# One queue of attention lines, the compression's small networks as its steps, and 128-row operands from the compressed probabilities

## Chip, cores and metric

One core of one Trainium2 chip. The metric is the device time of one execution in microseconds (us); the table below has the three runs of the kernel before.

## The reference

Two layers on 256 tokens of width 1024, all in float32. A layer is a gated feed-forward, an attention block, a second feed-forward and a small gated addition, each with an RMS norm ahead:

```python
h = h + 0.5 * swiglu(rms_norm(h, norm_g[i, 0]), ffn1_wi[i], ffn1_wo[i])
n = rms_norm(h, norm_g[i, 1])
... = split_cols(n @ w_in[i], IN_SPLITS)
ya = diff_attention(...)      # A: 4 heads, difference of two softmaxes
yb = nsa_attention(...)       # B: 8 heads in 2 groups, below
yc = swa_sink_attention(...)  # C: 8 heads in 2 groups, window 128, sinks
merged = (sigmoid(ga) * (ya @ w_branch[i, 0]) + sigmoid(gb) * (yb @ w_branch[i, 1])
          + sigmoid(gc) * (yc @ w_branch[i, 2]))
h = h + merged @ w_out[i]
```

Attention B has three parts that its gates sum: attention over compressed keys (15 blocks of 32 tokens at stride 16), over selected blocks (here all of them) and over a window. The compression is a small network, for keys and for values:

```python
def compress(t, pos, w1, w2):
    ...                                        # blocks of 32 tokens, + pos
    return jax.nn.gelu(blk @ w1) @ w2          # 15 rows of 64 a group
p_c = masked_softmax(s_c, dist_c >= 0)
o_c = einsum('bgrqn,bngd->bqgrd', p_c, v_cmp)  # joins o_s and o_w by gates
```

## The kernel before

**Products.** Every large product (`product`, L275) has the tokens, turned, as the stationary operand (128 x 128) and the weights as the moving one (128 x 512), with both split into a high and a low part: three matmuls a step (`mul3`, L218). Weights come in sub-blocks of 128 x 1024 through one queue (`Weights`, `fetch`, `load`, L232 to L264): a DMA, ScalarE's copy to `wh` (L212), VectorE's difference to `wl` (L207). Four raw buffers and six pairs of `wh` and `wl` go round.

**Lines beside the products.** The attentions A, C and B are generators, cut into steps by `yield`. `Flow` (L152) holds one of them. Each step of a product ends in `flow.tick()`, which adds the line's pace (0.75, 0.6, 0.7 for A, C, B; L33) and lets as many steps of the line be written as have come due. `flow.join` writes what is left. So a line's instructions stand between the product's in program order. A planner in the framework then sets each engine's order: by program order, but it takes a later instruction where an earlier one isn't ready by its reckoning. On the chip each engine's order is fixed.

**Order of a layer's attention block** (L873 to L896): projections A0, A1, A2; line A starts; projections Ck, Cq, Bk (16 ticks each); join; line C starts; Bv, Bq (16 each); branch 0, that is for each half c of the output columns a gate product (16 ticks) and a branch product (8); join; line B starts; `compress` (L604, 32 ticks); branch 2 the same way as branch 0; branch 1 with both gates first, then a join, then both branch products; then `wo`.

**Line B** (`attend_b`, L712) has six units: for tokens t = 0 the groups g = 0 and 1, for t = 1 each group twice (selected, window). `first` makes scores (L439), softmax (L448, L450) and scaling (L742); `second` turns the probabilities (L227), splits them into `pT` (L212, L207) and multiplies with the values (`weighted`, L664 and L665); `gather` (L669 to L676) adds halves and writes `yB`. The first and second of neighbouring units alternate (`pipelined`, L464). Ahead of the first second of each t stands `attend_cmp` (L680), whose turned probabilities `pcT` (L706 to L709, 16 rows) and compressed values `vc` (L654 to L659, 16 rows) make the last product of each g and t (L748). While `kc` is missing the line's steps are empty (L735).

**compress** makes 64 matmuls with `w1` (L624, L625), copies the sums to `c_sb` (L628), folds (L631), and runs the GELU and the second layer (L632 to L660) at one go, with `w2` from the weights' queue.

Of the kernel before, what the change touches and what calls it, by code (L numbers as in the profile page):

```python
# [10 lines left out]
F32 = mybir.dt.float32  # L11
# [123 lines left out]
def _constants():  # L135
    u = np.arange(REV)
    dist = 255 - u
    n = np.maximum(dist, 0)
    nf = np.maximum(n, 1).astype(np.float32)
    big = 16 + (np.log(nf / np.float32(16)) / np.float32(math.log(MAXDIST / 16)) * np.float32(16)).astype(np.int32)  # L140
    bucket = np.where(n < 16, n, np.minimum(big, BUCKETS - 1))
    onehot = (bucket[None, :] == np.arange(BUCKETS)[:, None]).astype(np.float32)
    dead = np.zeros((NB, REV), np.float32)
    dead[:, dist < 0] = NEG
    dead[12:, dist >= 128] = NEG
    ql, t, m = np.arange(128)[:, None, None], np.arange(2)[None, :, None], np.arange(16)[None, None, :]
    cmask = ((128 * t + ql - 16 * m - 31 >= 0) & (m < 15)).astype(np.float32).reshape(128, 32)
    return {"onehot": onehot, "dead": dead, "cmask": cmask, "ident": np.eye(128, dtype=np.float32),
            "fold": np.tile(np.eye(32, dtype=np.float32), (2, 1))}


class Flow:  # L152


    def __init__(self):
        self.side, self.pace, self.due = None, 0.0, 0.0

    def start(self, side, pace):
        self.side, self.pace, self.due = side, pace, 0.0

    def tick(self):
        if self.side is not None:
            self.due += self.pace
            while self.due >= 1.0:
                self.due -= 1.0
                if next(self.side, self) is self:
                    self.side = None
                    return

    def join(self):  # L170
        if self.side is not None:
            for _ in self.side:
                pass
            self.side = None


@with_exitstack
def trunk(ctx: ExitStack, tc: tile.TileContext, a: dict, out: bass.AP, index: list):
# [228 lines left out]
    def attention(i, norm, after):  # L407
# [193 lines left out]
        w1 = w2 = None  # L601
        kc, vc = [None], [None]

        def compress():  # L604
# [14 lines left out]
            for kv in range(2):  # L619
                for k in range(16):  # L620
# [5 lines left out]
                    flow.tick()  # L626
            c_sb = stage()
            nc.vector.tensor_copy(c_sb[:64], c_ps[:64])  # L628
            g_ps = tp_bank("gl")[:, :128]
            for k in range(4):  # L630
                nc.tensor.matmul(g_ps[:, 32 * k:32 * k + 32], c_sb[:64, 128 * k:128 * k + 128], fold, start=True, stop=True)  # L631
            gl = pool.tile([128, 128], F32, name="gl")  # L632
            nc.scalar.activation(gl, g_ps, AF.Square)
            nc.vector.tensor_scalar(gl, gl, 0.044715, 1.0, op0=ALU.mult, op1=ALU.add)
            nc.vector.tensor_tensor(gl, gl, g_ps, op=ALU.mult)
            nc.scalar.activation(gl, gl, AF.Tanh, scale=math.sqrt(2.0 / math.pi))
            nc.vector.tensor_scalar(gl, gl, 0.5, 0.5, op0=ALU.mult, op1=ALU.add)
            nc.vector.tensor_tensor(gl, gl, g_ps, op=ALU.mult)
            hid = pool.tile([128, 2, 128], F32R, name="hid")
            split(hid[:, 0], hid[:, 1], gl)  # L640
            w2h, w2l = w2(0)
            k_ps = tp_bank("kc")
# [8 lines left out]
            kt = pool.tile([128, 2, 2, 32], F32R, name="kc")  # L651
            split(kt[:, 0], kt[:, 1], kbd)
            v_ps = tp_bank("vc")
# [26 lines left out]
        def attend_cmp(t):  # L680
# [31 lines left out]
        def attend_b():  # L712
            bnd, y_ps = {}, {}

            def first(u):
# [107 lines left out]

        def branch(b, yT, last=False):

# [50 lines left out]
        yield project("A2", done_av)  # L876
        yield lambda: flow.start(attend_a(), PACE_A)
# [57 lines left out]
    fold = base.tile([64, 32], F32, name="fold")  # L935
    cmask = base.tile([128, 2, 16], F32, name="cmask")
    nsink = base.tile([128, DEPTH, 8], F32, name="nsink")
    nlam = base.tile([128, DEPTH], F32, name="nlam")
# [13 lines left out]
    def setup(pool):  # L952
# [14 lines left out]
        for g in range(2):  # L967
# [90 lines left out]
```

## Time and profile before

| what | value |
|---|---|
| runs, us | 1377.45, 1379.99, 1382.30; median 1379.99 |
| profiled execution, us | 1380.55 |
| its span, us | 1378.8 |
| TensorE (PE) busy | 1356.1 us, 98% of the span, 6598 matmuls |
| VectorE (DVE) busy | 882.2 us, 64% |
| ScalarE (ACT) busy | 779.1 us, 57% |
| granted TensorE clock, mean | 0.993 of full speed |
| HBM traffic | 183 GB/s over the span |

The profiled execution is one run. Its span goes from the first to the last instruction, and 1.75 us of its time lie around the span. Matmuls are pipelined, so that a record (0.39 us for a 128 x 512 product) is longer than the distance from one start to the next; costs are read from start to start. The attention block of layer 0 goes from 200 to 460 us; that of layer 1 repeats it 679 us later.

### The profile page before, as it was taken

How to read it: one execution, taken by the hardware profiler on the slowest of the kernel's cores; microseconds unless marked ns; L12 is line 12 of the kernel's file. 1: busy time of each engine (PE TensorE's matmuls, PEld its weight loads, DVE VectorE, ACT ScalarE, POOL GpSimd, SP SyncE). 2: the span in 40 equal slices, each digit the busy share in tenths (PEclk: the TensorE clock that was granted, in tenths of full speed). 3: DMA queues.
4: the chain of work that ended last, by engine and by line, in shares of the span. 5: the costliest groups of instructions: out<-in, count | busy, mean ns of one | idle time of the engine just before them, and what ended most of it. 6: DMA issues, size and time to landing. Idle time of an engine off the chain costs nothing.

```text
span 1378.8 us, 18265 instructions
## 1 busy us (share of the span) xinstructions
PE 1356.1 (98%) x6598; PEld 1111.2 (81%) x6598; DVE 882.2 (64%) x1585; ACT 779.1 (57%) x1377; POOL 19.1 (1%) x37
## 2 busy tenths in 40 slices
PE   7999999999999999999999999999999999999997
PEld 5888888887877888888888888888887778888886
DVE  6546556778877755555665555667697876555564
ACT  7535445668655644444654544566785656444454
POOL 0000000000000000000000000000000000000000
PEclk9999999999999999999999999999999999999999
DMA  8587566345634555555555555744546434555462
GB/s 284 189 268 241 192 205 211 122 160 169 223 119 137 165 186 184 183 173 187 199 183 183 183 183 176 243 157 132 169 164 221 139 123 166 195 183 188 161 205 87
DMA packets 74152, 249.53 MB, mean 181 GB/s; under 512 B 8720, under 2 KB 14276, under 8 KB 73934
## 3 DMA queue, kind: packets, MB, share of 16 engines
q1 hardware_dynamic: 73598, 243.36, 52.8%
q0 software_dynamic: 464, 5.01, 1.1%
q8 instruction: 52, 0.85, 0.2%
q14 instruction: 38, 0.31, 0.1%
HBM read 247.26 MB, written 5.01 MB: 183 GB/s over the span
## 4 chain that ended last, share of the span: by engine, by line
PE 92%; DMA 3%; DVE 3%; ACT 2%; issue 1%; SPq 0%; DVEq 0%; POOLq 0%; POOL 0%; ACTq 0%
PE ff L221 11%; PE ff L219 11%; PE ff L220 11%; PE fo L220 6%; PE fo L219 6%; PE fo L221 6%; PE gate L219 3%; PE gate L220 3%; PE gate L221 3%; DMA raw<-in_wst 2%; PE s L439 2%; PE br L219 2%; PE A L219 2%; PE A L220 2%; PE A L221 2%; PE br L221 2%
## 5 line engine op out<-in xcount | busy, mean ns | idle before, releaser
L207 DVE TENSOR_TENSOR wl<-raw,wh 128x1024 fp32r<-128x1024 f32 (+1 forms) x452 | 543.2, 1207 | 212.2 <-ACT wh L212 197.4
L212 ACT ACTIVATE wh<-raw 128x1024 fp32r<-128x1024 f32 (+1 forms) x452 | 471.0, 1046 | 218.1 <-PE fo L221 83.3
L219 PE MATMUL ff<-wh,nT 128*128 128x512 f32 x704 | 281.5, 400 | 6.7 <-ACT wh L212 6.7
L221 PE MATMUL ff<-wh,nT 128*128 128x512 f32 x704 | 277.6, 395 | 0.0
L220 PE MATMUL ff<-wl,nT 128*128 128x512 f32 x704 | 275.8, 392 | 0.0
L219 PEld LDWEIGHTS ff<-wh,nT 128*128 128x128 f32 x704 | 133.0, 189 | 33.7 <-ACT wh L212 7.4
L221 PEld LDWEIGHTS ff<-wh,nT 128*128 128x128 f32 x704 | 132.9, 189 | 27.5
L220 PEld LDWEIGHTS ff<-wl,nT 128*128 128x128 f32 x704 | 133.2, 189 | 26.9 <-DVE wl L207 0.9
L220 PE MATMUL fo<-wl,gT 128*128 128x512 f32 x352 | 134.3, 393 | 0.0
L221 PE MATMUL fo<-wh,gT 128*128 128x512 f32 x352 | 133.5, 390 | 0.0
L219 PE MATMUL fo<-wh,gT 128*128 128x512 f32 x352 | 133.3, 390 | 0.0
L388 ACT ACTIVATE act<-ff,stats 128x256 f32<-128x256 f32 x88 | 41.6, 473 | 159.1 <-PE ff L221 159.1
L389 DVE TENSOR_TENSOR gated<-act,ff 128x256 f32<-128x256 f32 x88 | 36.6, 416 | 124.2 <-ACT act L388 124.1
L219 PE MATMUL gate<-wh,nT 128*128 128x512 f32 x192 | 79.6, 414 | 0.0
L220 PE MATMUL gate<-wl,nT 128*128 128x512 f32 x192 | 78.4, 408 | 0.8 <-DVE wl L207 0.8
L221 PE MATMUL gate<-wh,nT 128*128 128x512 f32 x192 | 77.8, 405 | 0.0
L219 PEld LDWEIGHTS fo<-wh,gT 128*128 128x128 f32 x352 | 66.1, 188 | 13.7
L220 PEld LDWEIGHTS fo<-wl,gT 128*128 128x128 f32 x352 | 66.1, 188 | 13.4
L221 PEld LDWEIGHTS fo<-wh,gT 128*128 128x128 f32 x352 | 66.1, 188 | 13.3
L450 ACT ACTIVATE p<-p,st 128x128 f32<-128x128 f32 (+1 forms) x128 | 56.7, 446 | 12.1 <-DVE st L448 12.0
L305 ACT ACTIVATE nT<-nt,ngt 128x128 fp32r<-128x128 f32 x112 | 32.0, 371 | 31.1 <-PE nt L227 31.1
L220 PEld LDWEIGHTS gate<-wl,nT 128*128 128x128 f32 x192 | 37.6, 196 | 9.7 <-DVE wl L207 1.5
(286 smaller groups left out, 1961.3 us busy)
## 6 DMA issues: line engine op xcount, KB each, us to landing
raw<-in_wst SPq DMA_DIRECT2D x436, 512.0 KB, 4.3
band<-rev SPq DMA_DIRECT2D x10, 512.0 KB, 5.3
rev<-table POOLq DMA_DIRECT2D x1, 3840.0 KB, 17.3
raw<-in_wst SPq DMA_DIRECT2D x8, 256.0 KB, 6.0
raw<-in_wbv SPq DMA_DIRECT2D x4, 420.0 KB, 3.2
xt<-in_xt SPq DMA_DIRECT2D x4, 256.0 KB, 4.4
h<-in_x SPq DMA_DIRECT2D x2, 512.0 KB, 6.3
band<-rev POOLq DMA_DIRECT2D x2, 512.0 KB, 5.9
```

Of the source, the lines that this page charges most:

```text
L207: nc.vector.tensor_tensor(o, x, y, op=ALU.subtract)
L212: nc.scalar.activation(hi, src, AF.Copy)
L219: nc.tensor.matmul(ps, xh, wh, start=start, stop=False)
L220: nc.tensor.matmul(ps, xh, wl, start=False, stop=False)
L221: nc.tensor.matmul(ps, xl, wh, start=False, stop=stop)
L305: nc.scalar.activation(T[:, 0, k + m, :], src[:, 128 * m:128 * m + 128], AF.Copy, scale=ngt[:, self.row, k + m:k + m + 1])
L388: nc.scalar.activation(act, ps[:, :256], AF.Silu, scale=norm.r(t))
L389: nc.vector.tensor_tensor(held[t][:, f % 2, :], act, ps[:, 256:], op=ALU.mult)
L439: nc.tensor.matmul(o, q[r, x, qb[m], t * 128:(t + 1) * 128], kk, start=x + y == 0, stop=x == 1)
L450: nc.scalar.activation(p[j], p[j], AF.Exp, bias=st[:, j:j + 1], scale=-1.0, accum_out=st[:, n + j:n + j + 1])
```

## The change

`Flow` holds a list of lines instead of one: a tick serves the first of the list, at that line's pace, and a started line waits behind the others. Line A isn't joined any more before C starts; each line is joined in its own branch, after the gate product of half 0 (in branch 1 after both gates). Line B starts after `compress` instead of before it. `compress` ends with the copy to `c_sb`; fold, GELU and second layer become the first nine steps of line B (`compressed`). `w2` leaves the weights' queue: it has a DMA of its own ahead of `compress` and its own tile. The compressed values are computed on 128 rows (head-major, eight heads of 16), the compressed probabilities are turned all eight heads at once, and for each g and t a new function `own` multiplies them with a mask of the head's rows and splits the result into a `pT` tile of 128 rows; that takes one step more for each g and t. Paces and buffers stay.

```diff
@@ constants
+    own = np.arange(8)[:, None] == np.array([4 * g + 2 * pr + par for g in range(2) for par in range(2) for pr in range(2)])
+    hmask = own.repeat(16, 0).astype(np.float32)
...
@@ class Flow
-        self.side, self.pace, self.due = None, 0.0, 0.0
+        self.sides, self.due = [], 0.0
     def start(self, side, pace):
-        self.side, self.pace, self.due = side, pace, 0.0
+        self.sides.append((side, pace))
+        return side
+    def step(self):
+        side = self.sides[0][0]
+        if next(side, self) is self:
+            self.sides.pop(0)
     def tick(self):
-        if self.side is not None:
-            self.due += self.pace
-            while self.due >= 1.0:
+        if self.sides:
+            self.due += self.sides[0][1]
+            while self.due >= 1.0 and self.sides:
                 self.due -= 1.0
-                if next(self.side, self) is self:
-                    self.side = None
-                    return
+                self.step()
-    def join(self):
-        if self.side is not None:
-            for _ in self.side:
-                pass
-            self.side = None
+    def join(self, side):
+        while any(s is side for s, _ in self.sides):
+            self.step()
@@ attention
+        def second_weights():
+            nonlocal w2
+            raw = base.tile([128, SUB], F32, tag="raw", bufs=RAWS, name="w2raw")
+            nc.sync.dma_start(raw[:, :384], a["w2"][i])
+            w2 = pool.tile([128, 2, 384], F32R, name="w2")
+            split(w2[:, 0], w2[:, 1], raw[:, :384])
@@ compress: ends with the copy; the rest becomes compressed(), with yields
-            c_sb = stage()
-            nc.vector.tensor_copy(c_sb[:64], c_ps[:64])
+            c_sb[0] = pool.tile([128, 512], F32, name="c_sb")
+            nc.vector.tensor_copy(c_sb[0][:64], c_ps[:64])
+        def compressed():
+            yield
...
+            yield
             v_ps = tp_bank("vc")
-            for g in range(2):
-                for f in range(2):
-                    s, n = slice(256 + 64 * f, 320 + 64 * f), slice(64 + 32 * f + 16 * g, 80 + 32 * f + 16 * g)
-                    mul3(v_ps[:16, 64 * g:64 * g + 64], hid[:, 0, n], hid[:, 1, n], w2h[:, s], w2l[:, s], f == 0, f == 1)
-            vc[0] = pool.tile([16, 2, 128], F32R, name="vc")
-            values(vc[0], v_ps[:16, :128], None)
+            rows_ = base.tile([128, 2, 2, 128], F32R, tag="stage", bufs=4, name="rows")
+            for f in range(2):
+                for x in range(2):
+                    nc.vector.tensor_copy(
+                        rows_[:, x, f].rearrange("p (g h n) -> p g h n", g=2, h=4),
+                        hid[:, x, 64 + 32 * f:96 + 32 * f].rearrange("p (g n) -> p g n", g=2)[:, :, None, :].to_broadcast([128, 2, 4, 16]))
+            yield
+            for f in range(2):
+                s = slice(256 + 64 * f, 320 + 64 * f)
+                mul3(v_ps[:, :64], rows_[:, 0, f], rows_[:, 1, f], w2h[:, s], w2l[:, s], f == 0, f == 1)
+            yield
+            vc[0] = pool.tile([128, 1, 128], F32R, name="vc")
+            values(vc[0], v_ps[:, :64], None)
@@ attend_cmp: the turning
-            for g in range(2):
-                ps = tp_bank("pct")
-                for par in range(2):
-                    for m in range(2):
-                        j = 2 * par + m
-                        nc.tensor.transpose(ps[:16, 128 * j:128 * j + 128], p[:, 4 * g + 2 * m + par, :], ident)
-                T = pool.tile([16, 2, 512], F32R, tag="pcT", bufs=2, name="pcT")
-                split(T[:, 0], T[:, 1], ps[:16])
-                pcT[t, g] = T
-                yield
+            ps = tp_bank("pct")
+            transposes(ps, [p.rearrange("p h n -> p (h n)")])
+            pcT[t] = pool.tile([128, 128], F32, tag="pcT", bufs=2, name="pcT")
+            nc.scalar.activation(pcT[t], ps[:, :128], AF.Copy)
+            yield
+        def own(t, g):
+            o = stage("own").rearrange("p (j q) -> p j q", j=4)
+            nc.vector.tensor_tensor(o, pcT[t][:, None, :].to_broadcast([128, 4, 128]),
+                                    hmask[:, 4 * g:4 * g + 4, None].to_broadcast([128, 4, 128]), op=ALU.mult)
+            T = pool.tile([128, 2, 4, 128], F32R, tag="pT", bufs=3, name="pcT")
+            split(T[:, 0], T[:, 1], o)
+            return T
@@ attend_b: begins with compressed(); no wait for kc; the last product
+            yield from compressed()
...
-                    while kc[0] is None:
-                        yield
...
-                    weighted(y_ps[g, t], vc[0][:, g], pcT[t, g], False, True)
+                    T = own(t, g)
+                    yield
+                    weighted(y_ps[g, t], vc[0][:, 0], T.rearrange("p x j q -> p x (j q)"), False, True)
@@ branch: the line's join moves into the branch that reads it
-                yield flow.join
+                yield lambda: flow.join(sides[side])
...
                     yield gated(c, both[c][0])
+                    if c == 0:
+                        yield lambda: flow.join(sides[side])
                     yield mixed(c, both[c][1])
@@ the order of steps
-        yield flow.join
-        yield lambda: flow.start(attend_c(), PACE_C)
+        yield lambda: start("c", attend_c(), PACE_C)
...
-        yield from branch(0, yA)
-        yield flow.join
-        yield lambda: flow.start(attend_b(), PACE_B)
+        yield from branch(0, yA, "a")
         w1 = streamed(i, "w1", 256)
-        w2 = Weights(384, [(a["w2"][i], 384)], 1)
+        yield second_weights
         yield compress
-        yield from branch(2, yC)
-        yield from branch(1, yB, True)
+        yield lambda: start("b", attend_b(), PACE_B)
+        yield from branch(2, yC, "c")
+        yield from branch(1, yB, "b", True)
@@ setup
+        nc.sync.dma_start(hmask, a["hmask"])
```

## Rows read from the trace of the kernel before

**Rows 1.** The page: busy time of each engine, and the chain's shares by engine.

```profile
PE 1356.1 (98%) x6598; PEld 1111.2 (81%) x6598; DVE 882.2 (64%) x1585; ACT 779.1 (57%) x1377; POOL 19.1 (1%) x37
...
PE 92%; DMA 3%; DVE 3%; ACT 2%; issue 1%; SPq 0%; DVEq 0%; POOLq 0%; POOL 0%; ACTq 0%
```

**Rows 2.** Windows: stretches of layer 0, compress to the last branch (columns in line one).

```profile
core 0: us, PE busy (x) PEld busy (x) DVE busy (x) ACT busy (x) POOL busy (x), PEclk, DMA share, GB/s
...
344.00:358.00 14.00, 12.86 (x97) 11.02 (x96) 13.71 (x43) 10.68 (x29) 0.00 (x0) 1.00 0.53 175
358.00:400.00 42.00, 42.00 (x220) 34.69 (x220) 34.06 (x70) 27.07 (x48) 0.00 (x0) 0.96 0.63 199
400.00:436.00 36.00, 36.00 (x183) 28.21 (x183) 25.58 (x65) 20.08 (x44) 0.00 (x0) 0.95 0.32 103
436.00:451.00 15.00, 14.79 (x67) 11.20 (x65) 11.82 (x19) 7.76 (x13) 0.00 (x0) 1.00 0.38 136
```

**Rows 3.** Timeline of PE, end of compress (start, duration; in brackets idle time, releaser).

```profile
355.25 0.50 PE L220 MATMUL gate<-wl,nT 128*128 128x512 f32 x1 [0.42 <-DVE wl L207]
...
357.87 1.07 PE L631 MATMUL gl<-fold,stage 64*128 64x32 f32 x8 [0.72 <-DVE stage L628]
...
360.28 0.63 PE L220 MATMUL gate<-wl,nT 128*128 128x512 f32 x1
360.70 0.63 PE L221 MATMUL gate<-wh,nT 128*128 128x512 f32 x1
```

**Rows 4.** Timeline of PE in Bv, where line A is joined.

```profile
279.32 0.41 PE L227 MATMUL pt<-ident,p 128*128 128x128 f32 x2 [0.83 <-DVE half L574]
```

**Rows 5.** Timeline of PE, scores and turned probabilities.

```profile
385.58 0.98 PE L439 MATMUL s<-kB,qB 64*128 64x256 f32 x12
386.49 0.50 PE L220 MATMUL gate<-wl,nT 128*128 128x512 f32 x1
...
388.92 1.04 PE L706 MATMUL pct<-ident,pc 128*16 128x128 f32 x8
389.79 0.60 PE L227 MATMUL pt<-ident,p 128*128 128x128 f32 x4
```

**Rows 6.** Timeline of PE, 16-row products between full products.

```profile
411.22 0.39 PE L665 MATMUL yb<-pT,vB 128*128 128x512 f32 x1
...
411.67 0.39 PE L665 MATMUL yb<-pT,vB 128*128 128x512 f32 x1
411.99 0.50 PE L664 MATMUL yb<-pcT,vc 16*128 16x512 f32 x1
412.33 0.39 PE L665 MATMUL yb<-pcT,vc 16*128 16x512 f32 x1
412.65 0.50 PE L219 MATMUL gate<-wh,nT 128*128 128x512 f32 x1
```

**Rows 7.** Timeline of PE, products of the compressed values, two neighbours.

```profile
370.70 0.19 PE L220 MATMUL vc<-wl,hid 128*16 128x64 f32 x1
370.73 0.20 PE L221 MATMUL vc<-wh,hid 128*16 128x64 f32 x1
```

**Rows 8.** Timeline of DVE, line B's softmax, splits, scaling, loads and gather.

```profile
425.84 0.42 DVE L448 CUSTOM_DVE_ANT_0 p<-s,band 128x256 f32<-128x256 f32 x1 [3.96 <-PE pt L227]
...
426.19 0.42 DVE L448 CUSTOM_DVE_ANT_0 p<-s,band 128x256 f32<-128x256 f32 x1
...
427.22 1.95 DVE L207 TENSOR_TENSOR pT<-pt,pT 128x512 fp32r<-128x512 f32 x3
...
430.44 1.14 DVE L742 TENSOR_SCALAR p<-p,st 128x256 f32<-128x256 f32 x4
431.50 3.48 DVE L207 TENSOR_TENSOR wl<-raw,wh 128x1024 fp32r<-128x1024 f32 x3
435.25 0.85 DVE L674 TENSOR_TENSOR yt<-yt,yb 64x256 f32<-64x256 f32 x2 [0.26 <-PE pt L227]
```

**Rows 9.** Timeline of PE, the wait in the last branch.

```profile
448.11 0.50 PE L219 MATMUL br<-wh,yB 128*128 128x512 f32 x1 [0.21 <-ACT yB L212]
```

More of the change, by code (lines that the diff above doesn't have):

```diff
@@ L147, in _constants @@
     cmask = ((128 * t + ql - 16 * m - 31 >= 0) & (m < 15)).astype(np.float32).reshape(128, 32)
-    return {"onehot": onehot, "dead": dead, "cmask": cmask, "ident": np.eye(128, dtype=np.float32),
+    own = np.arange(8)[:, None] == np.array([4 * g + 2 * pr + par for g in range(2) for par in range(2) for pr in range(2)])
+    hmask = own.repeat(16, 0).astype(np.float32)
+    return {"onehot": onehot, "dead": dead, "cmask": cmask, "hmask": hmask, "ident": np.eye(128, dtype=np.float32),
             "fold": np.tile(np.eye(32, dtype=np.float32), (2, 1))}
@@ L601, in attention @@
         w1 = w2 = None
-        kc, vc = [None], [None]
+        def second_weights():
[4 more added lines that the diff above has]
+            split(w2[:, 0], w2[:, 1], raw[:, :384])
+        kc, vc, c_sb = [None], [None], [None]
         def compress():
@@ L626, in compress @@
                     flow.tick()
-            c_sb = stage()
-            nc.vector.tensor_copy(c_sb[:64], c_ps[:64])
+            c_sb[0] = pool.tile([128, 512], F32, name="c_sb")
+            nc.vector.tensor_copy(c_sb[0][:64], c_ps[:64])
+        def compressed():
+            yield
             g_ps = tp_bank("gl")[:, :128]
             for k in range(4):
-                nc.tensor.matmul(g_ps[:, 32 * k:32 * k + 32], c_sb[:64, 128 * k:128 * k + 128], fold, start=True, stop=True)
+                nc.tensor.matmul(g_ps[:, 32 * k:32 * k + 32], c_sb[0][:64, 128 * k:128 * k + 128], fold, start=True, stop=True)
+            yield
             gl = pool.tile([128, 128], F32, name="gl")
@@ L638, in compress @@
             nc.vector.tensor_tensor(gl, gl, g_ps, op=ALU.mult)
+            yield
             hid = pool.tile([128, 2, 128], F32R, name="hid")
             split(hid[:, 0], hid[:, 1], gl)
-            w2h, w2l = w2(0)
+            yield
+            yield
+            w2h, w2l = w2[:, 0], w2[:, 1]
             k_ps = tp_bank("kc")
@@ L652, in compress @@
             split(kt[:, 0], kt[:, 1], kbd)
+            yield
             v_ps = tp_bank("vc")
-            for g in range(2):
-                for f in range(2):
-                    s, n = slice(256 + 64 * f, 320 + 64 * f), slice(64 + 32 * f + 16 * g, 80 + 32 * f + 16 * g)
-                    mul3(v_ps[:16, 64 * g:64 * g + 64], hid[:, 0, n], hid[:, 1, n], w2h[:, s], w2l[:, s], f == 0, f == 1)
-            vc[0] = pool.tile([16, 2, 128], F32R, name="vc")
-            values(vc[0], v_ps[:16, :128], None)
+            rows_ = base.tile([128, 2, 2, 128], F32R, tag="stage", bufs=4, name="rows")
[4 more added lines that the diff above has]
+                        hid[:, x, 64 + 32 * f:96 + 32 * f].rearrange("p (g n) -> p g n", g=2)[:, :, None, :].to_broadcast([128, 2, 4, 16]))
+            yield
+            for f in range(2):
+                s = slice(256 + 64 * f, 320 + 64 * f)
+                mul3(v_ps[:, :64], rows_[:, 0, f], rows_[:, 1, f], w2h[:, s], w2l[:, s], f == 0, f == 1)
+            yield
+            vc[0] = pool.tile([128, 1, 128], F32R, name="vc")
+            values(vc[0], v_ps[:, :64], None)
             kc[0] = kt
@@ L700, in attend_cmp @@
             yield
-            for g in range(2):
-                ps = tp_bank("pct")
-                for par in range(2):
-                    for m in range(2):
-                        j = 2 * par + m
-                        nc.tensor.transpose(ps[:16, 128 * j:128 * j + 128], p[:, 4 * g + 2 * m + par, :], ident)
-                T = pool.tile([16, 2, 512], F32R, tag="pcT", bufs=2, name="pcT")
-                split(T[:, 0], T[:, 1], ps[:16])
-                pcT[t, g] = T
-                yield
+            ps = tp_bank("pct")
+            transposes(ps, [p.rearrange("p h n -> p (h n)")])
+            pcT[t] = pool.tile([128, 128], F32, tag="pcT", bufs=2, name="pcT")
+            nc.scalar.activation(pcT[t], ps[:, :128], AF.Copy)
+            yield
+        def own(t, g):
[5 more added lines that the diff above has]
+            return T
         def attend_b():
             bnd, y_ps = {}, {}
+            yield from compressed()
             def first(u):
@@ L761, in second @@
                 if ss[-1] == 1:
-                    weighted(y_ps[g, t], vc[0][:, g], pcT[t, g], False, True)
+                    T = own(t, g)
+                    yield
+                    weighted(y_ps[g, t], vc[0][:, 0], T.rearrange("p x j q -> p x (j q)"), False, True)
                     gather(yB[t], y_ps[g, t], g)
@@ L821, in attend_c, with branch @@
             yield from pipelined([(g, t) for g in range(2) for t in range(NT)], first, second)
-        def branch(b, yT, last=False):
+        def branch(b, yT, side, last=False):
             def parts(c):
@@ L876, in attention, with start @@
         yield project("A2", done_av)
-        yield lambda: flow.start(attend_a(), PACE_A)
+        sides = {}
+        def start(name, side, pace):
+            sides[name] = flow.start(side, pace)
+        yield lambda: start("a", attend_a(), PACE_A)
         yield project("Ck", done_ck, 256)
@@ L936, in trunk @@
     cmask = base.tile([128, 2, 16], F32, name="cmask")
+    hmask = base.tile([128, 8], F32, name="hmask")
     nsink = base.tile([128, DEPTH, 8], F32, name="nsink")
```

## The prediction

> **What bounds the kernel now.** I read the page first, then the windows of the attention block, then PE's timeline through it. The page shows PE busy for 98% of the span and 92% of the chain, DVE at 64%, ACT at 57% [rows 1]. So a microsecond counts where PE loses it: as work, as a wait, or as a stretch at the lower clock. The windows show how little is lost. From 358 to 436 us PE is busy throughout, and in the last branch it idles 0.21 of 15 us [rows 2]. [...] At the end of compress PE waits 0.42 us for a weight difference and 0.72 us for the copy of the compression's sums [rows 3]. In Bv, where line A's rest is written out, it waits 0.83 us for a VectorE copy [rows 4]. [...] The second layer repeats the pattern, so all terms below are per layer and count twice.
>
> **Turning the probabilities.** Before, each t turns eight heads alone, 16 transposes a layer; eight of them take 389.79 - 388.92 = 0.87 us, 0.11 each [rows 5]. After, there are two transposes a layer. 14 x 0.11 = -1.5 us, pure PE work.
>
> **Products of 16 rows.** From the last full product ahead to the first behind a pair, three starts take 412.65 - 411.67 = 0.98 us [rows 6]. Three full products at 0.225 would take 0.68. There are four pairs a layer: 4 x 0.30 = -1.2. The bound on the other side is 0, if the new 128-row pair costs as much as the old one. I take -1.2, since the new pair has the form of the product ahead of it.
>
> [...]
>
> **Compressed values.** Twelve products before, 0.03 us apart [rows 7]; six after, with a full stationary operand: at the 0.11 of a transpose [rows 5], 0.66 against 0.36: +0.3. Four copies on DVE are new; they stand between two steps of the line and PE has gates meanwhile: 0.
>
> **End of compress.** The fold moves two steps of line B later, among the gates, so a late copy no longer stands in PE's way at once: -0.7. Line B's first softmax is now written behind compress, and DVE, 13.71 of 14 us busy there [rows 2], has less ahead of the copy and of the weight differences. I take half of the 0.42: -0.2. [...] Sum -1.7, bounds 0 (the planner may take the first unit's scores forward, and DVE stays full) and -2.8. Against it: w2's split now stands ahead of part of w1's on ACT and DVE, and its DMA ahead of theirs on SP; it was in the same queue a few loads later, so it shifts 0.4 of a load (384 of 1024 columns) and costs nothing while the next buffers are filled. B's two band DMAs on SP move behind w1's loads with its start; the first softmax that needs one stands ten steps into the gates, so they cost 0. Behind DVE's copies for the values wait at most the next weight difference.
>
> **Join of A gone.** Line A has 42 steps: each first gives five yields, each second t + 5, over four units. 48 ticks at 0.75 write 36. The seven calls left fall into the first 10 ticks of Bv, and C, with 37 calls at 0.6, ends about 71 of the 80 ticks on instead of 62, still ahead of compress. Half of the 0.83 us wait [rows 4] goes: -0.4, bounds 0 and -0.8.
>
> **The drain of B.** This is the cost. Before, line B has 72 steps: 34 in the firsts, 28 in the seconds, 10 in the two attend_cmp. 14 are written in compress, where the rest of its due steps are empty (no kc), and 80 ticks at 0.7 write 56: two are left at the join. After, it has 83: 9 of compressed and 4 of own more, 2 fewer turnings. None is written in compress. 56 due leaves 27 for the join: the scores and softmaxes of the last two units, the seconds of the last three. On PE these are two score groups at 0.91 [rows 5], six turnings of four transposes at 0.11, and 16 products at 0.225: 1.8 + 2.6 + 3.6 = 8.0 us. All the gates are behind them. What can fill: branch products of t = 0, two halves of 12, and half of those of t = 1, 36 x 0.225 = 8.1 us; some of these do so already now, ahead of the wait of [rows 9]. Together 16.1 us for PE. DVE has in the same stretch [rows 8] two softmaxes (4 x 0.35 and 1.14 of scaling, 5.1), six splits at 0.65 (3.9), two own with a multiplication and a split, priced like splits (2.6), two gathers (1.7), the mixing of t = 0, four operations priced at 0.65 (2.6), two weight differences at 1.16 (2.3): 18.2 us. DVE is the longer by 2.1, and PE waits for it. [...] Bounds: 0 (waits as now, 0.21), and +10, if the filling comes first and B's 8.0 us of PE then stand alone against the 18.2 of DVE.
>
> Neither the masks' multiplications elsewhere (two more a layer) nor the new DMA of 4 KB at the start reach PE: DVE is busy for 34.06 of 42 and 25.58 of 36 us in the gates' stretches [rows 2].
>
> **Sum.** -1.5 - 1.2 + 0.3 - 1.7 - 0.4 + 3.0 = -1.5 a layer, -3.0 in all: 1380.55 - 3.0 = 1377.5 against the profiled execution. That run lies 0.56 above the median of the three; against the median the forecast is 1377.0.
>
> **Rivals.**
> Drain that costs more (slower). DVE's order is fixed by the planner, and in the gates' stretch it stood 3.96 us for one transposition of a unit two back, with a softmax behind it [rows 8]; there PE had gates, in the drain it has none. Price: 2.1 + 4.0 and a whole half-speed stretch of 1.7 = 7.8 a layer against gains of 4.5: +3.3, 6.6 in all, which gives 1386.6 against the median. It decides from 4.5 us of PE's idle time a layer between the last gate and wo. For: the last three units hang on each other through three p buffers and one y bank. Against: PE waited 0.21 us there with the same order of kinds [rows 9].
> Drain hidden, stalls gone (faster). The planner takes scores of the last units forward into gates, as it took other work forward, and all waits of compress and Bv go: -1.5 - 1.2 + 0.3 - 2.8 - 0.8 = -6.0, -12 in all, which gives 1368. For: PE's fill between gates and wo is plentiful at first. Against: a gate is nearly always ready, so that nothing calls a later step forward.
> The change doesn't do what it says. The waits at compress and Bv are DVE's load, not the place in program order, and stay; the 128-row pairs cost as before: -1.5 + 0.3 + 2.1 = +0.9, 1.8 in all, which gives 1381.8.
>
> **How the numbers follow.** Forecast case 0.42, the costly drain 0.25, the hidden drain 0.23, no effect 0.10. About 0.3%, 4.1 us, is what a measurement here can tell from no change, so faster means under 1375.9, slower over 1384.1. Of the forecast's 0.42 I put 0.16 under the lower mark: faster 0.39. Same: 0.26 + 0.10 = 0.36. Slower 0.25. The range goes from a little under the hidden drain to a little over the costly one, 1367 to 1388; the forecast case alone is 1372 to 1382.
>
> **What would show it.** In the changed kernel: 4 transposes of pc in all; 0.23 between the starts around the last product of each g and t; the fold among the gates without a wait on c_sb; PE idle time between the last gate of branch 1 and wo, with releasers on DVE or ACT, near 2 us a layer, and DVE nearly full there. If that stretch shows over 4.5 us, or the clock falls in it for long, the forecast is wrong upward; if scores of the last units stand well before the last gates, wrong downward.

## The result, and the profile after

| | before | changed |
|---|---|---|
| median of 4 runs each, same chip, us | 1379.22 (1377.45 to 1382.30) | 1388.66 (1388.42 to 1389.61) |
| profiled span, us | 1378.8 | 1386.8 |
| ratio of the times | 1 | 1.0064, 95% interval 1.0047 to 1.0081 |

The change costs 0.64%. The forecast was 1377.0, with a range up to 1388.

The page of the changed kernel, against [rows 1]: busy us of each engine with its share of the span and its instructions, and the chain by engine.

```profile
PE 1347.6 (97%) x6558; PEld 1106.6 (80%) x6558; DVE 886.3 (64%) x1601; ACT 782.2 (56%) x1381; POOL 19.0 (1%) x37
...
PE 84%; DVE 6%; ACT 4%; DMA 4%; issue 2%; SPq 0%; DVEq 0%; POOLq 0%; POOL 0%; ACTq 0%
```

DVE's busy time has hardly moved. PE's share of the chain fell from 92 to 84%: other engines now end last in places where they did not.

The windows of layer 0, against [rows 2] (stretch, length, busy us and instructions of PE, PEld, DVE, ACT, POOL, then PE's mean clock). The last gate product starts at 424.94, `wo` at 455.75.

```profile
344.00:358.00 14.00, 13.10 (x92) 11.32 (x91) 13.88 (x42) 11.50 (x29) 0.00 (x0) 1.00 0.71 228
358.00:400.00 42.00, 39.87 (x195) 32.48 (x194) 32.09 (x63) 22.34 (x35) 0.00 (x0) 1.00 0.61 203
400.00:425.00 25.00, 25.00 (x126) 20.86 (x124) 18.90 (x41) 16.99 (x32) 0.00 (x0) 1.00 0.38 125
425.00:456.00 31.00, 25.68 (x132) 19.71 (x131) 24.90 (x61) 17.60 (x41) 0.00 (x0) 0.94 0.29 99
```

Three things differ. The stretch behind the last gate is 30.8 us long instead of 15.3, with 31.00 - 25.68 = 5.3 us of idle PE instead of 0.21, and a clock of 0.94. A window set on the stretch at the lower level shows 3.4 us of it, which lose 1.7 at half speed:

```profile
436.71:440.12 3.41, 3.41 (x14) 2.83 (x13) 3.19 (x8) 1.66 (x3) 0.00 (x0) 0.50 0.00 0
```

From 358 to 400 PE idles 2.1 us, where it idled not at all. And the two half-speed stretches of before, 0.96 from 358 and 0.95 from 400, are not there in this execution.

PE's timeline of the changed kernel in layer 0: the instructions that waited (idle time and releaser in brackets), in four places, and the fold, which did not.

```profile
280.24 0.41 PE L232 MATMUL pt<-ident,p 128*128 128x128 f32 x2 [1.04 <-DVE half L579]
282.00 0.63 PE L232 MATMUL qt<-ident,stage 128*128 128x128 f32 x4 [0.44 <-DVE stage L571]
...
325.28 0.50 PE L224 MATMUL gate<-wh,nT 128*128 128x512 f32 x1 [0.54 <-DVE merged L871]
...
354.64 0.50 PE L224 MATMUL gate<-wh,nT 128*128 128x512 f32 x1 [0.90 <-ACT wh L217]
...
358.94 0.50 PE L225 MATMUL gate<-wl,nT 128*128 128x512 f32 x1 [0.69 <-DVE wl L212]
360.52 1.07 PE L648 MATMUL gl<-fold,c_sb 64*128 64x32 f32 x8
...
371.19 0.50 PE L224 MATMUL br<-wh,yC 128*128 128x512 f32 x1 [1.44 <-ACT th L867]
...
435.45 0.50 PE L695 MATMUL yb<-pT,vB 128*128 128x512 f32 x1 [3.03 <-DVE pT L212]
443.01 0.47 PE L694 MATMUL yb<-pT,vB 128*128 128x512 f32 x1 [0.67 <-DVE yt L704]
452.56 0.50 PE L224 MATMUL br<-wh,yB 128*128 128x512 f32 x1 [1.53 <-ACT yB L217]
```

The fold has lost its wait of 0.72 us [rows 3], but two gate products ahead of it, which wait for their weights, and the first branch product for yC, which ScalarE's tanh of a gate (`th`) releases, cost 0.90 + 0.69 + 1.44. Bv waits 1.04 + 0.44 instead of 0.83 [rows 4] and 0.18, which is this line of the kernel before:

```profile
280.82 0.63 PE L227 MATMUL qt<-ident,stage 128*128 128x128 f32 x4 [0.18 <-DVE stage L566]
```

The largest single wait, 3.03, is behind the last gate. DVE's timeline shows what it did meanwhile (start, duration, instruction):

```profile
431.07 0.69 DVE L740 TENSOR_TENSOR own<-pcT,hmask 128x512 f32<-128x512 f32 x1
431.68 1.13 DVE L777 TENSOR_SCALAR p<-p,st 128x256 f32<-128x256 f32 x4
432.73 0.68 DVE L740 TENSOR_TENSOR own<-pcT,hmask 128x512 f32<-128x512 f32 x1
433.33 0.41 DVE L453 CUSTOM_DVE_ANT_0 p<-s,band 128x256 f32<-128x256 f32 x1
...
434.71 1.88 DVE L212 TENSOR_TENSOR pT<-pt,pT 128x512 fp32r<-128x512 f32 x3
```

Two maskings, a scaling and a softmax stand on DVE ahead of the difference that PE wants at 432. PE had turned the probabilities by then; of the branch products that need nothing more from line B, the planner had put 12 ahead, with starts from 426.2 to 428.8, and the next from 444.5 on. So for 15 us PE had only line B's own chain and one turning of `merged`.

From the first product of A to the first of the next feed-forward, layer 0 takes 279.5 us instead of 275.7, layer 1 also 279.5, instead of 276.1. Nearly all of the rest of the span's 8.0 us is 0.9 us ahead of layer 0's A, a start that lies between 200.5 and 205.2 us in the profiled runs whatever the kernel.

### The profile page after: what moved, and what is told of

Its sections match the earlier page's. It is cut to its first block, busy times and chain, and to the rows that moved or that the text cites. A ratio compares the mean times of both kernels' runs of the same rounds, so it can differ in the third digit from the quotient of the medians.

```text
span 1386.8 us, 18191 instructions
## 1 busy us (share of the span) xinstructions
PE 1347.6 (97%) x6558; PEld 1106.6 (80%) x6558; DVE 886.3 (64%) x1601; ACT 782.2 (56%) x1381; POOL 19.0 (1%) x37
## 4 chain that ended last, share of the span: by engine, by line
PE 84%; DVE 6%; ACT 4%; DMA 4%; issue 2%; SPq 0%; DVEq 0%; POOLq 0%; POOL 0%; ACTq 0%
PE ff L224 11%; PE ff L226 11%; PE ff L225 11%; PE fo L225 6%; PE fo L224 6%; PE fo L226 6%; DMA raw<-in_wst 3%; DVE wl L212 2%; PE gate L224 2%; PE gate L225 2%; PE gate L226 2%; PE A L224 2%; PE A L225 2%; PE A L226 2%; PE gt L232 1%
## 5 line engine op out<-in xcount | busy, mean ns | idle before, releaser
L224 PE MATMUL gate<-wh,nT 128*128 128x512 f32 x192 | 76.8, 400 | 2.8 <-ACT wh L217 1.7
L226 PE MATMUL gate<-wh,nT 128*128 128x512 f32 x192 | 75.3, 392 | 0.0
L224 PEld LDWEIGHTS gate<-wh,nT 128*128 128x128 f32 x192 | 36.1, 188 | 11.2 <-ACT wh L217 2.2
```

The costliest lines, as they stand in the source:

```text
L224: nc.tensor.matmul(ps, xh, wh, start=start, stop=False)
L226: nc.tensor.matmul(ps, xl, wh, start=False, stop=stop)
```

## The experiments

The kernel before ran beside each group of runs, with medians of 1378.69, 1380.47, 1381.58 and 1379.93. So ratios are compared here, not times. "Behind the last gate" means from the last gate product of branch 1 to `wo`, in layer 0. The turnings include the one of the compressed probabilities, which the expectations leave out (33 here, 32 there).

| run | line B behind the last gate: scores, turnings, products | length, us | PE idle, us | ratio to before | 95% interval |
|---|---|---|---|---|---|
| before | 0, 4, 10 | 15.3 | 0.2 | 1 | |
| changed | 24, 33, 20 | 30.8 | 5.3 | 1.0064 | 1.0047 to 1.0081 |
| e1 pace 1.0 | 0, 4, 10 | 15.4 | 0.4 | 1.0009 | 0.9998 to 1.0021 |
| e2 pace 0.85 | 12, 20, 19 | 26.4 | 3.5 | 1.0070 | 1.0055 to 1.0085 |
| e3 before, pace 0.39 | 24, 40, 20 | 30.6 | 2.3 | 1.0078 | 1.0062 to 1.0094 |
| e4 before, 128 rows | 0, 8, 14 | 18.6 | 2.1 | 0.9979 | 0.9965 to 0.9993 |
| e5 A ahead of C | 0, 24, 20 | 24.2 | 3.7 | 1.0005 | 0.9992 to 1.0017 |
| e6 w2 behind | 0, 24, 20 | 24.2 | 3.7 | 1.0011 | 0.9999 to 1.0023 |
| e7 inline | 0, 0, 10 | 16.0 | 1.5 | 1.0013 | 1.0000 to 1.0026 |
| e8 e4 at pace 0.78 | 0, 12, 16 | 21.3 | 2.3 | 0.9991 | 0.9977 to 1.0006 |
| e9 e5 + e6 | 0, 4, 10 | 15.3 | 0.4 | 0.9946 | 0.9928 to 0.9964 |
| e12 mask on GpSimd | 24, 33, 20 | 29.9 | 5.8 | 1.0086 | 1.0060 to 1.0112 |
| e13 e9, mask on GpSimd | 0, 4, 10 | 15.4 | 0.4 | 0.9948 | 0.9931 to 0.9966 |
| e14 e4, mask on GpSimd | 0, 4, 10 | 16.5 | 1.5 | 0.9957 | 0.9942 to 0.9973 |
| e15 e9 at pace 0.7 | 24, 33, 20 | 30.8 | 5.3 | 1.0025 | 1.0006 to 1.0043 |

### The drain alone: e1, e2, e3

Theory D: the steps of line B that are left at its join cost what PE waits behind the last gate. Rival O: the loss lies elsewhere. e1 and e2 change the pace of the changed kernel, e3 that of the kernel before.

```diff
-PACE_A, PACE_B, PACE_C = 0.75, 0.7, 0.6
+PACE_A, PACE_B, PACE_C = 0.75, 1.0, 0.6     # e1; 0.85 in e2, 0.39 in e3
```

> The changed kernel with line B's pace at 1.0 instead of 0.7: 80 ticks write 80 of its 83 steps, so 3 are left at the join instead of 27. Theory D (the loss is the steps of line B left at the join, about 6.4 us of PE time a layer between the last gate and wo): 1375 us (1372 to 1379), PE idle time in that stretch under 1.5 us a layer. Rival O (the loss is own's extra multiplications and splits on DVE and ACT, and the waits at compress and ahead of the branch products of yC, wherever the steps stand): 1386 to 1390.

1379.49 us, ratio 1.0009, half a microsecond over theory D's range and far from rival O's. The drain is gone: the windows of e1 at compress and behind the last gate show 0.40 us idle in the last 16.

```profile
344.00:358.00 14.00, 12.57 (x91) 10.99 (x89) 13.36 (x41) 11.64 (x29) 0.00 (x0) 1.00 0.69 238
...
435.00:451.00 16.00, 15.60 (x71) 12.17 (x70) 12.61 (x19) 8.35 (x13) 0.00 (x0) 1.00 0.41 128
```

Against the changed kernel that is 0.55%, 7.6 us. The rest of the forecast's gain did not show: the first row has 1.4 us of idle PE at compress, so the other terms need runs of their own.

> The changed kernel with line B's pace at 0.85: 68 due, 15 steps left at the join. Theory D: between the changed kernel and the run with pace 1.0, near 1381 us (1378 to 1385), since the drain is about halved. Rival O: 1386 to 1390.

1388.47 us, ratio 1.0070: theory D as put there missed. With 15 steps left in place of 27, the loss stayed. The window from the last gate to `wo` of e2:

```profile
430.00:457.00 27.00, 23.50 (x108) 17.54 (x107) 19.14 (x40) 14.54 (x29) 0.00 (x0) 0.94 0.34 115
```

3.5 us idle, and a clock of 0.94 over these 27 us, which is half-speed time as in the changed kernel. The number of steps left does not set the price.

> The kernel before, with nothing but line B's pace lowered from 0.7 to 0.39: 12 steps written in compress and 31 in the 80 ticks leave 28 of 72 at the join, as many as the change leaves. Theory D: the same drain without any of the change's other parts, 1391 us (1387 to 1396). Rival O: 1378 to 1382, since no work is added.

1389.81 us, ratio 1.0078, as D had it. A late line B alone, with nothing of the change, costs about 11 us. In layer 0 only 2.1 us of that is idle PE behind the last gate; with all idle time and the lower clock taken out, its block is still 2.7 us longer than before, for the same matmuls in another order. The window of e3 behind the last gate and its longest wait:

```profile
428.00:459.00 31.00, 28.66 (x140) 20.63 (x139) 23.40 (x57) 17.66 (x40) 0.00 (x0) 0.95 0.28 100
...
454.01 0.50 PE L219 MATMUL br<-wh,yB 128*128 128x512 f32 x1 [1.45 <-ACT yB L212]
```

### The 128-row operands alone: e4, e8, e14

e4 puts `own`, the mask, the one turning and the values for 128 rows into the kernel before, and leaves its queue, its `compress` and its pace.

```diff
-                        nc.tensor.transpose(ps[:16, 128 * j:128 * j + 128], p[:, 4 * g + 2 * m + par, :], ident)
+            transposes(ps, [p.rearrange("p h n -> p (h n)")])
...
-                    weighted(y_ps[g, t], vc[0][:, g], pcT[t, g], False, True)
+                    T = own(t, g)
+                    yield
+                    weighted(y_ps[g, t], vc[0][:, 0], T.rearrange("p x j q -> p x (j q)"), False, True)
```

> The kernel before with the 128-row operands alone (own, the values on 128 rows, one turning for eight heads); lines, joins, compress and w2's queue as before, 4 steps left at the join. Theory D: PE work falls by 2.4 us a layer and the rest is hidden, 1374 us (1371 to 1378). Rival O: own's work on DVE and ACT costs as much as it saves on PE or more, 1378 to 1386.

1376.46 us, ratio 0.9979: within what was expected. Behind the last gate PE idles 2.1 us here, up from 0.2 to 0.8, so the operands give more than the total shows. In e8 only the pace differs:

```diff
-PACE_A, PACE_B, PACE_C = 0.75, 0.7, 0.6
+PACE_A, PACE_B, PACE_C = 0.75, 0.78, 0.6
```

> The kernel before with the 128-row operands alone (one turning for eight heads, masks, products of 128 rows), and line B's pace 0.78 instead of 0.7, so that no step is left at the join. At 0.7 its trace shows PE waiting 1.7 us for yB and 0.36 us for pT behind the last gate in each layer. Theory D (what is left at the join is paid behind the last gate): these 2.0 us a layer go: 1372.5 (1370 to 1375). Rival (the chain of the last unit is exposed at any pace, or DVE pays elsewhere): 1375 to 1378.

1378.99 us, ratio 0.9991: missed. No step is left at the join, and yet the planner put more behind the last gate than at 0.7: 12 turnings and 16 products, against 8 and 14. The window of e8 there:

```profile
429.00:451.00 22.00, 19.71 (x84) 15.20 (x84) 16.15 (x25) 11.36 (x20) 0.00 (x0) 0.92 0.39 134
```

e14 leaves the pace and moves the mask's multiplication from DVE to GpSimd, which changes the planner's order (4 turnings and 10 products behind the last gate):

```diff
-            nc.vector.tensor_tensor(o, pcT[t][:, None, :].to_broadcast([128, 4, 128]),
+            nc.gpsimd.tensor_tensor(o, pcT[t][:, None, :].to_broadcast([128, 4, 128]),
```

> The kernel before with the 128-row operands alone, pace 0.7, and the mask's multiplication on GpSimd. With VectorE's multiplication PE's order had 14 products and 8 turnings behind the last gate and PE waited 2.1 us there; with GpSimd's it has 10 and 4, as in the kernel before. Theory P: the wait falls to 0.4 to 0.8 us, 1.5 us a layer less: 1373.5 (1371.5 to 1376). Rival (GpSimd's multiplication is late for the products that need it): 1376 to 1380.

1374.67 us, ratio 0.9957, as theory P had it, though 1.5 us of idle PE stay behind the last gate, not 0.4 to 0.8.

### A's tail, w2 and the steps: e5, e6, e7, e9

All four stand on e1, so at pace 1.0.

```diff
+        yield lambda: flow.join(sides["a"])        # e5, e9: line A's rest first
         yield lambda: start("c", attend_c(), PACE_C)
...
-        yield second_weights
         yield compress
+        yield second_weights                       # e6, e9
```

> The changed kernel with the faster pace of line B (1.0), and line A's rest written out before line C starts, as in the kernel before. With the faster pace alone PE waits per layer 1.05 + 0.45 us in Bv, 0.55 us ahead of branch 0's second gate, 1.0 to 1.4 us at the end of compress, 0.69 us ahead of the second product of the first gate and 1.0 to 1.2 us for yC. Theory Q (the one queue makes the waits, since line C starts later and its tail moves into compress): the waits at Bv, at the gate and at the end of compress go back to those of before, about 2 us a layer less: 1375.5 (1373 to 1378). Rival V (VectorE's load in compress makes them, whichever line it comes from): the same within 1 us a layer, 1377.5 to 1381.

> The changed kernel with pace 1.0, and w2's load and split written behind compress instead of ahead of it, so that on SP, ACT and DVE they stand behind all of w1's that compress asks for. Theory W (w2 ahead of w1's last loads takes a raw buffer and a place on DVE, and so delays the weights that compress and the gate behind it wait for): the waits of 1.4, 0.7 and 1.0 us at the end of compress and at yC shrink by half or more, 1.5 us a layer: 1376.5 (1374 to 1378). Rival V (DVE's load, the place of w2 does not matter): within 0.5 us a layer, 1378.5 to 1380.5.

1381.25 and 1381.83 us, ratios 1.0005 and 1.0011. By their totals both look like rival V. The traces say otherwise. In e5 Bv waits 0.85 and 0.18 us, as before, and neither branch 0's second gate nor the gates at compress wait; 2.08 us are left at yC. In e6 the waits of 1.43 and 0.69 us at compress are gone, and 1.03 us stay at yC, as do those in Bv. So either edit alone takes the waits at compress away. What was won came back behind the last gate, where both orders have 24 turnings and 20 products instead of 4 and 10. The window of e5 at compress, and those of e6 at compress and behind the last gate:

```profile
344.00:358.00 14.00, 14.00 (x103) 12.35 (x104) 12.09 (x35) 11.24 (x28) 0.00 (x0) 1.00 0.54 177
```

```profile
344.00:358.00 14.00, 14.00 (x97) 12.07 (x95) 13.92 (x37) 12.08 (x30) 0.00 (x0) 1.00 0.63 211
...
426.00:450.00 24.00, 20.26 (x98) 15.21 (x97) 19.59 (x41) 13.91 (x28) 0.00 (x0) 1.00 0.33 106
```

e7 undoes the steps: the small networks are written out at once behind compress, and line B has pace 0.9.

```diff
-            yield from compressed()
...
         yield compress
+        yield lambda: [None for _ in compressed()]
```

> The changed kernel with the compression's small networks written out at once behind compress, as before, not as steps of line B; line B's pace 0.9, which for its 74 steps leaves 2 at the join, as in the kernel before. Theory S (the steps take the wait for the fold's operand out of PE's way, as the prediction had it): the fold's operand is waited for again, 0.7 us or more a layer, against 1.0 pace with steps at 1379.5: 1381 (1380 to 1383). Rival V (the planner takes steps forward anyway and DVE is full there): the same within 0.5 us a layer, 1378.5 to 1380.5, or less, if the steps themselves lengthen the way to the compressed keys.

1381.68 us, ratio 1.0013 against e1's 1.0009: no difference. (The time alone lies in theory S's range, but the kernel before was also 1.8 us slower beside this run than beside e1.) The fold's operand is not waited for in e7 either; the gate ahead of it waits, 1.16 us against e1's 1.43. So the steps are not what took that wait away: the gates beside it pay in both.

> The changed kernel with pace 1.0 and both edits that took waits away one by one: line A's rest written out before line C starts, and w2 written behind compress. PE's own order here leaves 10 products of line B and 4 turnings behind the last gate, as in the kernel before; each edit alone left 20 and 24. Theory P (what counts is what the planner leaves behind the last gate, not the number of steps left at the join): about 0.4 us of waits there instead of 3.7, 1.0 us in Bv, none ahead of branch 0's second gate, about 1 us at the end of compress; against pace 1.0 alone 3 us a layer less: 1373.5 (1371 to 1376.5). Rival G (what is not lost at compress is lost behind the last gate, whatever the order, since DVE is short): 1379 to 1382.

1373.20 us, ratio 0.9946: theory P. The planner's order is the short one again, and the waits that e5 and e6 removed stay away. This is faster than both kernels. Its windows from compress on, and its two waits in Bv, to be held against the changed kernel's:

```profile
340.00:354.00 14.00, 14.00 (x98) 11.91 (x96) 12.07 (x31) 11.31 (x28) 0.00 (x0) 1.00 0.52 173
354.00:396.00 42.00, 41.44 (x216) 33.60 (x216) 35.81 (x78) 25.19 (x44) 0.00 (x0) 1.00 0.72 237
396.00:433.00 37.00, 37.00 (x197) 29.61 (x196) 31.79 (x82) 25.86 (x56) 0.00 (x0) 1.00 0.31 101
433.00:449.00 16.00, 15.62 (x71) 12.19 (x70) 12.61 (x19) 8.37 (x14) 0.00 (x0) 1.00 0.37 130
```

```profile
281.67 0.41 PE L232 MATMUL pt<-ident,p 128*128 128x128 f32 x2 [0.85 <-DVE half L579]
283.17 0.63 PE L232 MATMUL qt<-ident,stage 128*128 128x128 f32 x4 [0.18 <-DVE stage L571]
```

0.56 us of idle PE in 93 us up to 433, 0.38 behind it, and in this execution the upper clock throughout.

### Whether the two costs add, and whether DVE's masking is the cause: e15, e12, e13

e15 is e9 with the changed kernel's pace, 0.7. It fills the fourth corner: drain kept, A's tail and w2 put right.

> The changed kernel at its own pace of line B (0.7), with line A's rest written ahead of line C and w2 behind compress: the fourth corner of a square whose others are the changed kernel (ratio 1.0064 to the kernel before), pace 1.0 alone (1.0009) and both (0.9946). PE's order leaves 24 scores, 32 turnings and 20 products behind the last gate, as in the changed kernel. Theory 2 (two costs that lie in different stretches and add: the drain behind the last gate, and A's tail with w2 ahead of the weights): 1.0064 - (1.0009 - 0.9946) = 1.0001, 0.998 to 1.002. Rival G (what is not lost at compress is lost behind the last gate while that is long): 1.005 to 1.008.

1382.81 us, ratio 1.0025. The sum of the other corners is 1.0001, with their intervals some 0.003 wide either way; theory 2's range ended at 1.002, just below, and rival G's 1.005 lies outside this run's interval. So rival G is out, and the two costs add within what this measurement tells. The edits save 0.39% at pace 0.7 and 0.63% at pace 1.0, so that part of their gain may still hang on the drain. Behind the last gate of layer 0 e15 repeats the changed kernel's 5.3 us and its clock (in layer 1 it has 2.9 us of waits there, in the same order):

```profile
424.00:455.00 31.00, 25.68 (x133) 19.84 (x132) 24.92 (x61) 17.57 (x40) 0.00 (x0) 0.94 0.27 90
```

e12 puts e14's edit into the changed kernel, e13 into e9.

> The changed kernel, unchanged in pace (0.7), with the mask's multiplication of the compressed probabilities on GpSimd instead of VectorE; PE's order behind the last gate is that of the changed kernel (24 scores, 32 turnings, 20 products). Theory O (the 3.03 us wait of the changed kernel behind the last gate is VectorE's: two maskings and their differences stand ahead of the turned probabilities): 1.5 to 3 us a layer less there: 1384 (1382 to 1386). Rival C (the chain of the units, not VectorE's load, sets the wait, or GpSimd's multiplication is slow itself): 1387 to 1391.

1391.55 us, ratio 1.0086: theory O missed. PE still waits for the turned probabilities (3.3 us now), since the scaling and the softmax still stand ahead of them on DVE, and the scaling takes 2.71 us instead of 1.13 while GpSimd multiplies (below). That DVE's maskings were the cause of the 3.03 us is not borne out; without GpSimd at work beside the scaling it wasn't tried.

> The kernel with pace 1.0, A's rest ahead of C, w2 behind compress, and the mask's multiplication on GpSimd. PE's order behind the last gate is the short one (10 products, 4 turnings). If theory P holds for the first of these runs, VectorE's 4 x 0.6 us a layer lie beside other work and this run is within 1.5 us of it; if VectorE's load sets the time in the stretch of the gates, 1 to 2 us a layer less; if GpSimd's multiplication is slow, 1 to 2 us a layer more.

1373.80 us, ratio 0.9948, the same as e9. With gates for PE beside it, the masking costs nothing on either engine.

## Why the prediction was wrong

The step that failed is the drain of B, which was mis-sized; the terms for the end of compress and the join of A had the wrong sign. The terms, per layer, in the prediction's order, against the traces of layer 0 (one execution of each kernel):

| term | forecast | measured |
|---|---|---|
| turning, products of 16 rows, compressed values | -1.5 - 1.2 + 0.3 = -2.4 | about -2.5 (the rest of the account) |
| waits at the end of compress, yC with them | -0.9 | +1.9 (0.42 + 0.72 to 0.90 + 0.69 + 1.44) |
| half-speed stretch behind compress | -0.8 | -1.7 |
| half-speed stretch from 400 | none | -1.7 |
| join of A | -0.4 | +1.0 (0.83 + 0.18 to 1.04 + 0.44, and 0.54 ahead of a gate) |
| drain of B | +3.0 | +6.8 (5.3 - 0.2 of waits, 1.7 of clock) |
| sum | -1.5 | +3.8 |

The two half-speed stretches before are 3.4 us long and lose 1.7 each, which is the 1.7 in the price of the rival "drain that costs more". Windows set on them, with the clock at 0.50:

```profile
359.43:362.84 3.41, 3.41 (x10) 2.65 (x8) 3.13 (x3) 2.48 (x4) 0.00 (x0) 0.50 0.74 207
403.80:407.20 3.40, 3.40 (x11) 2.67 (x9) 2.85 (x13) 2.44 (x10) 0.00 (x0) 0.50 0.50 154
```

Two parts of the forecast's sum were the author's estimates of the clock, and no run shows what they rest on, that waits of PE bring the lower clock. They are 0.8 of the -1.7 for the end of compress and 0.9 of the +3.0 for the drain. The changed kernel waits longer than before at compress, 0.90 + 0.69, and has a clock of 1.00 from 358 to 400. Behind the last gate it has 3.4 us at 0.50 after the wait of 3.03, but e12 has 1.00 after one of 3.3.

**PE's work** was right for this order. The product price of 0.225, half of 411.67 - 411.22 [rows 6], has its row in the changed kernel's timeline of PE:

```profile
448.78 0.39 PE L695 MATMUL yb<-pT,vB 128*128 128x512 f32 x1
449.01 0.40 PE L694 MATMUL yb<-pcT,vc 128*128 128x512 f32 x1
449.24 0.39 PE L695 MATMUL yb<-pcT,vc 128*128 128x512 f32 x1
449.47 0.39 PE L224 MATMUL br<-wh,yB 128*128 128x512 f32 x1
```

Three starts take 0.69 us where they took 0.98 [rows 6]: 0.29 a pair, nearly the 0.30 that was taken. So 128 rows cost less here than 16 between 128-row neighbours. What the operands save hangs on the order around them too: with idle time and the lower clock taken out, layer 0's block is 2.5 us shorter than before in the changed kernel and 2.7 in e4, but only 0.8 in e9.

**The drain** is the term that decided, and it was mis-sized. Its step set PE's 16.1 us against DVE's 18.2 and took the difference as the wait. That treats the two engines as if each could always work on what it has. The rows show that neither is full there (25.7 and 24.9 of 31 us): PE waits in DVE's fixed order and in the chain of the last units, and the branch products that should have filled the holes had been placed ahead of or behind them. The amounts for PE were about right (forecast: two score groups, 24 turnings, 16 products; found: 24 scores, 33, 20); DVE's were too small, 18.2 us against 24.9. The rival "drain that costs more" had the mechanism (a planned order on DVE, no gates beside it), the place, and nearly the price: 7.8 a layer against 6.8, from 4.5 us of idle PE; it was 5.3. It was given 0.25, less than it deserved: its "against" was the wait of before [rows 9], read in a stretch with 2 steps left. Taken away by the pace alone, the drain gave back 3.8 us a layer between medians (e1). The clock doesn't make this difference: executions at the same mean clock, 0.996, take 1379.3 and 1380.2 us in e1 and, on another chip, 1388.4 to 1388.7 in the changed kernel.

**End of compress and join of A** went the other way. The premise was that line B's first softmax is written behind compress and so leaves DVE. The planner takes it forward as it did: line B's scores of three units (36 matmuls) run over the same stretch, in the kernel before and in the changed one (summary of the tile `s`: count, ns, first and last start):

```profile
L439 PE MATMUL s<-kB,qB x36: 274/278/384, 321.9 to 351.6; 64*128 64x256 f32 x36
```

```profile
L444 PE MATMUL s<-kB,qB x36: 274/278/384, 322.8 to 350.6; 64*128 64x256 f32 x36
```

DVE stays full at compress (13.88 of 14 us, 13.71 before [rows 2]), as the rival "the change doesn't do what it says" had it. But a full DVE isn't what makes PE wait there: in e6 it is busy for 13.92 of 14 us and PE never waits. w2's split was put at nothing, "while the next buffers are filled"; with line A's tail beside line C it isn't nothing. Written behind compress (e6), w2 lets the waits of the two gates go; with w2 left ahead and line A's tail put ahead of C (e5), they go as well. So at pace 1.0 it takes both to make these waits. And line A's tail beside the start of C, counted as a gain, costs waits in Bv and ahead of a gate, which go in e5 and e9.

With both undone, and a pace that leaves no drain, the kernel takes 0.54% less than before, some 1372 on the first chip, near the 1368 of the rival "drain hidden". That nearness is in part luck, as the windows of layer 0's whole block show, before and in e9:

```profile
200.54:476.22 275.68, 273.05 (x1467) 223.16 (x1466) 207.96 (x477) 179.20 (x389) 3.89 (x6) 0.99 0.50 164
```

```profile
202.89:473.95 271.06, 268.81 (x1448) 220.30 (x1447) 210.31 (x485) 180.35 (x391) 3.88 (x6) 1.00 0.50 167
```

Of the 4.6 us between them 3.4 are the two half-speed stretches (1.7 each), which this execution of e9 hasn't, 0.4 are waits, and 0.8 is left for PE's work, where the rival counted 2.4.

**The range** ended at 1388 because the costly drain was joined to all the gains at compress and Bv. That these gains would fail stood in another rival; that the waits there would grow, by 2.9 us a layer, stood in none. 1388.66 is both at once, less 3.4 us a layer of clock, of which 0.8 was counted.

Still open: why a later or earlier pace makes the planner leave more behind the last gate (e8 against e4, e5 and e6 against e1). The rows show that it does, not why. It is open too how much of e9's gain is its order and how much the granted clock (below). Whether the edits of e5 and e6 are both needed once the drain is short wasn't run apart from each other.

## What to carry to other kernels

A line of small work beside large products was cheapest here while they covered it: pace 1.0 against 0.7 gave 7.6 us. Behind the last of them its price is that of its chain and of the fixed order on each engine, not the difference of two engines' busy times. After an edit to such a line, count in the new order what stands behind the last covering product before reading anything else: twice here a saved wait came back there, and both times the total alone would have condemned a good edit. A step that is written later leaves an engine only if the planner doesn't take it forward; whether it does is to be seen in the trace of before.

## What the runs showed of the hardware

DVE's scalings took longer beside GpSimd. In e12 four scalings of 128 x 256, 1.13 us together in the changed kernel, took 2.71 while GpSimd ran its two multiplications; the next four, with GpSimd idle, took 1.14 (timelines of POOL and DVE of e12):

```profile
432.85 2.11 POOL L740 TENSOR_TENSOR own<-pcT,hmask 128x512 f32<-128x512 f32 x2 [26.85 <-ACT pcT L734]
```

```profile
432.67 2.71 DVE L777 TENSOR_SCALAR p<-p,st 128x256 f32<-128x256 f32 x4
...
438.87 1.14 DVE L777 TENSOR_SCALAR p<-p,st 128x256 f32<-128x256 f32 x4
```

The first four began 0.2 us ahead of GpSimd and ended 0.4 behind it, and were 1.6 us longer beside 2.11 of GpSimd; by what mechanism no run shows. Two maskings take GpSimd 2.04 and 2.11 us in e12, 2.15 and 2.92 in e14; one takes DVE 0.69 in the changed kernel.

The lower clock came and went with the order in the profiled executions: two stretches among the gates before, where PE was busy throughout [rows 2]; in the changed kernel one, behind the wait of 3.03 us; none from 340 us to `wo` in e9. Each of these is 3.4 us long and costs 1.7, as much as a long wait. But the order doesn't fix it. In layer 0 of e12 the wait of 3.3 us stands in the same place, and the clock stays at the upper level behind it:

```profile
426.00:457.00 31.00, 25.20 (x136) 19.06 (x135) 25.95 (x60) 18.46 (x41) 2.11 (x2) 1.00 0.30 101
```

Executions of one kernel differ as well: beside the experiments the kernel before ran at mean clocks from 0.990 to 0.998 and took 1374.1 to 1385.0 us, the longest time at 0.990 and the shortest at 0.998. So a part of a difference between two kernels can be clock. Between the medians of e9 and of the kernel before beside it (mean clocks 0.9975 and 0.993) lie 8.4 us; between executions at the same mean clock, 0.996 to 0.998, some 3.5, with only three such executions of the kernel before. What sets the clock among busy gates stays open.
